# The first mixer: where POOL splits the query weights of the third and fourth group

## The chip, the core and the metric

The kernel runs on one core of a Trainium2 chip. The metric is device time in microseconds (us), the median of several executions. The engines are TensorE (PE in the profile, with its weight loads as PEld), VectorE (DVE), ScalarE (ACT), GpSimd (POOL) and SyncE (SP), whose queue issues the DMAs.

## The reference

The kernel computes two layers of an encoder trunk on 512 tokens of width 1024, in float32. Each layer is a token mixer with 12 heads in three key/value groups, beside 4 heads of attention to 256 memory tokens, and then a gated feed-forward part. The first layer's mixer is the banded one, with a sink logit per head:

```python
def reference(x, mem, ...):
    mem_n = rms_norm(mem, mem_norm_g)
    for i in range(DEPTH):
        h = rms_norm(x, g_mix_pre[i])
        proj = h @ w_in[i]                     # q | k | v | q for the memory heads
        ...
        tok = mixer_a(q, k, v, attn_sink[0], cos_p, sin_p)   # i = 0: |i - j| <= 128
        mkv = mem_n @ w_mem_kv[i]
        mo = memory_attention(qm, km, vm)
        o = jnp.concatenate([tok, mo], axis=-1) @ w_o[i]
        x = x + rms_norm(o, g_mix_post[i])
        h = rms_norm(x, g_ffn_pre[i])
        gu = h @ w_gate_up[i]
        f = (jax.nn.silu(gu[..., :D_FF]) * gu[..., D_FF:]) @ w_down[i]
        x = x + rms_norm(f, g_ffn_post[i])
    return x
```

In `mixer_a` the queries and keys get a rotary embedding on 16 of 64 dimensions, the scores get a band mask, and the softmax's denominator has the term of the sink.

## The kernel before

Every product of float32 matrices is made from three products of numbers split into a high part (rounded to TensorE's fp32r format) and a low part, the rest. A weight is loaded into a raw tile of 128 x 1024 by SP (`raw`, three buffers), and `split` makes `whi` (a copy in fp32r) and `wlo` (raw less `whi`), each with four buffers. `split` is told by a number of two bits who does it: with the bit of value 2 set POOL makes the high part (L284), else ScalarE (L286); with the bit of value 1 set POOL makes the low part (L288), else VectorE (L290). The table PACE holds these bits. For the query weights of the first layer they are `'qw': [0, 0, 0, 1, 3, 3, 3, 3]`, two entries for each of four groups of four heads: the halves of the third group and of the fourth (the four memory heads) are split by POOL alone, each in four instructions of 128 x 512, two copies and two subtractions (NPART is 2, so a half comes in two parts).

TensorE's order is fixed by hand. `mixer` puts each piece of work into a list with a position, in units of heads, and runs the list in that order. Head number hg has its four scores at hg, hg + 1/4 and so on, its turns (`turn`, transposes of the probabilities, L643) 1.69 later, and the products with the values (`value`, L657 and L658) half a head after these. The query products of groups 1 to 3 begin at 4c - 5 plus a small offset, that is at -0.8, 3.1 and 7.1. The other engines' instructions are ordered by the scheduler of the framework, by priority and by when their operands are expected.

For a head, VectorE adds the mask and takes the maximum (L588), ScalarE makes the exponentials `p` (L594), and `normalise` adds the sink's term to the denominator (L629, VectorE), takes the reciprocal `rd` (L630, VectorE) and multiplies the four pieces of `p` with it on POOL (L633). The turns wait for that. Between these instructions VectorE makes the rotary embedding of the next group's queries (`rope_a`: L440, L442 and L443, 128 x 64 elements each, with both inputs in SBUF), and the low part of these queries (L290, `q`). Before the heads, the memory's keys are made: `mem_pieces` leaves them in `k2`, POOL makes a second copy of the high part (`again`, L417), and `keys` transposes them for TensorE (L424, L429) with copies out of PSUM by ScalarE (L426) and VectorE (L430, `kmb`).

The raw tiles are used in turn, so that SP's load of a later unit waits until the split of the unit three places ahead is done (L230); SP's queue is in program order.

Of the kernel before, what the change touches and what calls it, by code (L numbers as in the profile page):

```python
# [13 lines left out]
OP = mybir.AluOpType  # L14
# [16 lines left out]
NPART = 2  # L31
WPART = 2
BIG = 1e37
NFILL = 3
URGENT = 150
FIRST = ((0, 0.05, 0.1, 0.15, 1, 1.5), (0.5, 0.55, 0.6, 0.65, 1.25, 1.75))
LATE = {2: 1.2, ("r", 0): 1.05, ("r", 1): 1.3, 3: 2.2, ("r", 2): 2.4, ("r", 3): 3.4, ("m", 0): 4.5, ("m", 1): 5,
        "rows": 4, ("rm", 0): 6, ("rm", 1): 6.2}
# [147 lines left out]
class Trunk:  # L186
    def __init__(self, tc, a):
        self.tc, self.nc, self.a, self.nraw, self.more, self.early = tc, tc.nc, a, 0, None, {}
        self.pairs, self.todo, self.stores = {}, [], []

    def pool(self, stack, name, side="left", **kw):
        return stack.enter_context(self.tc.tile_pool(name=name, bufs=1, side=side, reuse_waits="tile", **kw))
# [16 lines left out]
                                       for z in range(2)]  # L209
            self.stores = [(self.pairs[(name, *at)][z], pair[z].bitcast(F32)) for z in range(2)]  # L210

    def unit(self, src, side=0, pool=None, parts=1, put=None, x=0, dst=None, key=None, g=None, raw=None, pair=None, early=None):


        nc, n = self.nc, src.shape[-1]
        own = raw or self.early.pop(early, None)
        if pair in self.pairs:
            def fetch():
                dst[key] = [self.whl.tile([P, 1024], F32R, tag=z, name=f"w{z}", bufs=4) for z in ("hi", "lo")]
                for z in range(2):  # L220
                    nc.sync.dma_start(dst[key][z].bitcast(F32), self.pairs[pair][z])

            put(x, fetch)
            return

        def load():
            raw = own or self.raw()
            hi, lo = [(pool or self.whl).tile([P, 1024], F32R, tag=z, name=f"w{z}", bufs=4) for z in ("hi", "lo")]
            if not own:
                nc.sync.dma_start(raw[:, :n], src)  # L230
            return raw, hi, lo

        def part(t, c0, c1):
            raw, hi, lo = t
            if g is None:
                self.split(hi[:, c0:c1], lo[:, c0:c1], raw[:, c0:c1], side)
                return
            m = n // g.shape[1]
            for k in range(c0 // m, c1 // m):
                c = slice(k * m, k * m + m)  # L240
                if side & 1:
                    nc.gpsimd.tensor_scalar(raw[:, c], raw[:, c], g[:, k:k + 1], 1.0, op0=OP.mult, op1=OP.mult)
                else:
                    self.split_scaled(hi[:, c], lo[:, c], raw[:, c], g[:, k:k + 1], side)
            if side & 1:
                self.split(hi[:, c0:c1], lo[:, c0:c1], raw[:, c0:c1], side)

        if put is None:
            t = load()
            for z in range(parts):  # L250
                part(t, z * n // parts, (z + 1) * n // parts)
            return t[1:]
        box = []

        def first():
            box.append(load())
            dst[key] = box[0][1:]
            part(box[0], 0, n // NPART)

        put(x, first)  # L260
        for z in range(1, NPART):
            put(x + z / 4, lambda z=z: part(box[0], z * n // NPART, (z + 1) * n // NPART))

    def raw(self):

# [27 lines left out]
    def urgent(self):  # L293

        return self.tc.high_priority(URGENT)

# [219 lines left out]
    def q_pieces(self, l, c, qTs, put, x0, lead):  # L516
        nc = self.nc
        w = {}
        for z in range(2):
            self.unit(self.a["wq"][l, c, z], self.side(l, "qw", 2 * c + z), put=put, x=x0 - lead + z * lead / 3, dst=w,  # L520
                      key=z, pair=("wq", l, c, z), early=("wq", z) if l == c == 0 else None)

        def prod(t, st, u):
            self.ready(t)
# [98 lines left out]
    def normalise(self, hd):  # L623
        nc, sink, nm, den = self.nc, hd["sink"], hd["nm"], hd["den"]
        rd = self.small.tile([P, 4], F32, tag="rd", name="rd", bufs=4)
        if sink is not None:
            es = self.small.tile([P, 4], F32, tag="es", name="es", bufs=3)
            nc.scalar.activation(es, nm, AF.Exp, bias=self.sink[:, sink:sink + 1], scale=1.0)
            nc.vector.tensor_add(den, den, es)  # L629
        nc.vector.reciprocal(rd, den)  # L630
        for z, (k0, k1) in enumerate(hd["rng"]):
            n = (k1 - k0) * P
            self.pooled = nc.gpsimd.tensor_scalar(hd["p"][z][:, :n], hd["p"][z][:, :n], rd[:, z:z + 1], 1.0,  # L633
                                                  op0=OP.mult, op1=OP.mult)

    def turn(self, hd, j):
        nc = self.nc
# [45 lines left out]
    def mixer(self, l, mkp, late, tokp):  # L683
# [9 lines left out]
        def put(x, f):  # L693
            bisect.insort(items, (x, next(count), f), key=lambda z: (-z[0], -z[1]))
# [48 lines left out]
        for z, key in enumerate(list(late)):  # L743
            at = pc["late"] + z - (len(late) - 1) if l else LATE[key]
            put(xk + at * k, lambda key=key: self.ready(key))
        lay(self.kv_pieces(l), xk, k, pc["klag"], lambda t: 0 if l else max(0, t - 1) / 4, None if l else FIRST)
        lay(self.q_pieces(l, 0, qT, put, xq + pc["q0off"], pc["q0lead"]), xq + pc["q0off"], pc["q0step"], pc["q0lag"],
# [621 lines left out]
```

## Time and profile before

| | us |
|---|---|
| median of 3 runs | 1112.88 |
| lowest and highest run | 1111.99, 1113.64 |
| the profiled execution | 1110.48 |
| its span, first to last instruction | 1108.7 |
| TensorE busy | 1089.4 |
| VectorE busy | 840.7 |
| ScalarE busy | 658.5 |
| POOL busy | 196.2 |

The granted clock of TensorE is 0.999 over the span. The profiled execution took 1.78 us more than its span, and lies 2.40 us below the median of the runs. The first mixer's heads begin at about 56 us of the span and end at about 170. In the profile's lines, `x4` is the number of merged instructions, the arrow in brackets names what ended the idle time ahead of an instruction, and `L288` is a line of the kernel before.

### The profile page before, as it was taken

The numbers are of one execution on the slowest core, as the hardware profiler recorded it, in microseconds if no ns is written. First come the engines' busy times: TensorE is split into PE (matmuls) and PEld (weight loads), VectorE is DVE, ScalarE is ACT, GpSimd is POOL, SyncE is SP. The second block draws the span as 40 slices with busy tenths as digits, with TensorE's granted clock in tenths as the row PEclk, the third lists the DMA queues.
The fourth block names the chain that finished last, engine by engine and source line by source line (L and its number), as shares of the span: only waits on it lengthen the run. The fifth ranks groups of instructions, "written<-read, shape, count | busy, mean of one in ns | idle before, by whom it ended". The sixth has DMA issues, their size and how long they took to land.

```text
span 1108.7 us, 19514 instructions
## 1 busy us (share of the span) xinstructions
PE 1089.4 (98%) x7438; PEld 1000.2 (90%) x7438; DVE 840.7 (76%) x1433; ACT 658.5 (59%) x1356; POOL 196.2 (18%) x342
## 2 busy tenths in 40 slices
PE   8999999999999999999999999999999999999997
PEld 7989978999889989998898888879999899899986
DVE  7789875999558767875788988758995478669854
ACT  6679975765445534563567888756664366346631
POOL 5683331102000000000443542212000000000001
PEclk9999999999999999999999999999999999999999
DMA  8621017343833472325543221145136123322243
GB/s 319 224 98 40 25 33 266 115 153 127 308 116 108 152 248 76 115 92 189 186 143 114 77 77 38 39 172 171 59 112 213 56 95 115 134 72 98 82 168 114
DMA packets 40558, 142.44 MB, mean 128 GB/s; under 512 B 4624, under 2 KB 5008, under 8 KB 40336
## 3 DMA queue, kind: packets, MB, share of 16 engines
q1 hardware_dynamic: 40176, 140.66, 36.8%
q8 instruction: 58, 0.95, 0.4%
q10 hardware_dynamic: 288, 0.53, 0.2%
q14 instruction: 36, 0.29, 0.1%
HBM read 122.30 MB, written 18.87 MB: 127 GB/s over the span
## 4 chain that ended last, share of the span: by engine, by line
PE 88%; DVE 5%; ACT 2%; POOL 2%; issue 1%; DMA 1%; DVEq 0%; POOLq 0%; SPq 0%; ACTq 0%
PE ps L277 14%; PE ps L276 14%; PE ps L278 14%; PE ps L1042 12%; PE ps L1041 12%; PE ps L1040 12%; PE tp L643 3%; PE o L658 2%; PE o L657 2%; PE s L582 1%; PE s L583 1%; DVE tl L290 1%; POOL r L310 1%; DVE tok L666 1%; ACT junk L314 1%
## 5 line engine op out<-in xcount | busy, mean ns | idle before, releaser
L286 ACT ACTIVATE whi<-raw 128x1024 fp32r<-128x1024 f32 (+3 forms) x205 | 168.5, 839 | 176.9 <-PE ps L1042 73.5
L290 DVE TENSOR_TENSOR wlo<-raw,whi 128x1024 fp32r<-128x1024 f32 (+3 forms) x202 | 190.9, 960 | 73.5 <-ACT whi L286 71.5
L1041 PE MATMUL ps<-sf,wlo 128*128 128x256 f32 x640 | 179.8, 281 | 0.0
L1040 PE MATMUL ps<-sf,whi 128*128 128x256 f32 x640 | 179.7, 281 | 0.0
L1042 PE MATMUL ps<-sf,whi 128*128 128x256 f32 x640 | 179.7, 281 | 0.0
L276 PE MATMUL ps<-whi,f 128*128 128x512 f32 (+1 forms) x360 | 138.7, 385 | 0.0
L277 PE MATMUL ps<-wlo,f 128*128 128x512 f32 (+1 forms) x360 | 138.5, 385 | 0.0
L278 PE MATMUL ps<-whi,f 128*128 128x512 f32 (+1 forms) x360 | 138.4, 385 | 0.0
L1042 PE MATMUL ps<-a,whi 128*128 128x256 f32 x480 | 134.4, 280 | 0.0
L1040 PE MATMUL ps<-a,whi 128*128 128x256 f32 x480 | 134.4, 280 | 0.0
L1041 PE MATMUL ps<-a,wlo 128*128 128x256 f32 x480 | 133.8, 279 | 0.0
L1041 PEld LDWEIGHTS ps<-sf,wlo 128*128 128x128 f32 x640 | 121.4, 190 | 0.5
L1040 PEld LDWEIGHTS ps<-sf,whi 128*128 128x128 f32 x640 | 121.1, 189 | 0.5
L1042 PEld LDWEIGHTS ps<-sf,whi 128*128 128x128 f32 x640 | 121.4, 190 | 0.0
L319 POOL TENSOR_SCALAR e<-sso 128x1 f32<-128x1 f32 x8 | 3.4, 420 | 563.9 <-ACT junk L314 563.7
L276 PE MATMUL ps<-whi,hT 128*128 128x256 f32 (+1 forms) x312 | 95.2, 305 | 0.0
L633 POOL TENSOR_SCALAR p<-p,rd 128x256 f32<-128x256 f32 (+2 forms) x128 | 76.5, 615 | 101.0 <-DVE rd L630 43.2
L277 PE MATMUL ps<-wlo,hT 128*128 128x256 f32 (+1 forms) x312 | 91.1, 292 | 2.9 <-DVE wlo L290 2.9
L278 PE MATMUL ps<-whi,hT 128*128 128x256 f32 (+1 forms) x312 | 90.9, 291 | 0.0
L1041 PEld LDWEIGHTS ps<-a,wlo 128*128 128x128 f32 x480 | 90.5, 188 | 0.2
L1040 PEld LDWEIGHTS ps<-a,whi 128*128 128x128 f32 x480 | 90.4, 188 | 0.2
L1042 PEld LDWEIGHTS ps<-a,whi 128*128 128x128 f32 x480 | 90.1, 188 | 0.0
(209 smaller groups left out, 2703.6 us busy)
## 6 DMA issues: line engine op xcount, KB each, us to landing
raw<-in_wgu_dram SPq DMA_DIRECT2D x48, 512.0 KB, 4.3
raw<-in_wd_dram SPq DMA_DIRECT2D x44, 512.0 KB, 4.4
rb<-in_wgu_dram SPq DMA_DIRECT2D x40, 512.0 KB, 3.6
raw<-in_wo_dram SPq DMA_DIRECT2D x17, 512.0 KB, 3.7
raw<-in_wq_dram SPq DMA_DIRECT2D x16, 512.0 KB, 5.3
xt<-x SPq DMA_DIRECT2D x12, 512.0 KB, 4.7
raw<-in_wm_dram SPq DMA_DIRECT2D x8, 512.0 KB, 4.0
x<-y SPq DMA_DIRECT2D x8, 512.0 KB, 3.0
```

The lines of the kernel that those rows point to most:

```text
L276: mm(out, lh, rh, start=first, stop=False)
L277: mm(out, lh, rl, start=False, stop=False)
L278: mm(out, ll, rh, start=False, stop=last)
L286: a = nc.scalar.activation(hi, src, AF.Copy)
L290: b = nc.vector.tensor_sub(lo, src, hi.bitcast(F32))
L633: self.pooled = nc.gpsimd.tensor_scalar(hd["p"][z][:, :n], hd["p"][z][:, :n], rd[:, z:z + 1], 1.0, op0=OP.mult, op1=OP.mult)
L643: nc.tensor.transpose(tp[:, z], hd["p"][i][:, jj * P:(jj + 1) * P], self.ident)
L657: nc.tensor.matmul(o[:, c0:c1], hd["v"](j), th, start=(j == 0), stop=False, skip_group_check=True)
L658: nc.tensor.matmul(o[:, c0:c1], hd["v"](j), tl, start=False, stop=last, skip_group_check=True)
L1040: mm(out, wh[:, s], rh, start=start and k == 0, stop=False, skip_group_check=True)
L1041: mm(out, wl[:, s], rh, start=False, stop=False, skip_group_check=True)
L1042: mm(out, wh[:, s], rl, start=False, stop=k == 3, skip_group_check=True)
```

## The change

The splits of the four halves are each tied to a normalising: the third group's halves come behind that of heads 0 and 1, and the fourth group's behind that of heads 3 and 4. `normalise` keeps its last POOL instruction of every head, and both parts of a half are issued within `issue_after` of that instruction, which sets the order of the two and does no more. Only the first layer has entries.

```diff
+BEHIND = {(0, 2, 0): 0, (0, 2, 1): 1, (0, 3, 0): 3, (0, 3, 1): 4}
...
+        def behind(c0, c1):
+            with nullcontext() if after is None else self.tc.issue_after(self.pooled[after].ins):
+                part(box[0], c0, c1)
+
         def first():
             box.append(load())
             dst[key] = box[0][1:]
-            part(box[0], 0, n // NPART)
+            behind(0, n // NPART)
 
         put(x, first)
         for z in range(1, NPART):
-            put(x + z / 4, lambda z=z: part(box[0], z * n // NPART, (z + 1) * n // NPART))
+            put(x + z / 4, lambda z=z: behind(z * n // NPART, (z + 1) * n // NPART))
...
-                      key=z, pair=("wq", l, c, z), early=("wq", z) if l == c == 0 else None)
+                      key=z, pair=("wq", l, c, z), early=("wq", z) if l == c == 0 else None, after=BEHIND.get((l, c, z)))
...
-            self.pooled = nc.gpsimd.tensor_scalar(hd["p"][z][:, :n], hd["p"][z][:, :n], rd[:, z:z + 1], 1.0,
-                                                  op0=OP.mult, op1=OP.mult)
+            self.pooled[hd["hg"]] = nc.gpsimd.tensor_scalar(hd["p"][z][:, :n], hd["p"][z][:, :n], rd[:, z:z + 1], 1.0,
+                                                            op0=OP.mult, op1=OP.mult)
```

In the changed kernel every line behind the new table is a few lines further on. The first place is POOL's queue at the first heads. `k2_824` and `k2_855` are the two tiles of memory keys; `raw_1083` and `raw_1134` the halves of the third group's weights; `rd_941` and `rd_1035` the reciprocals of heads 0 and 1. Before:

```order
L417 TENSOR_SCALAR k2_824<-k2_824 128x4x64 [waits DVE_49,Activation_49]
L284 TENSOR_SCALAR whi_1084<-raw_1083 128x512 [waits DMAHW4_49]
L284 TENSOR_SCALAR whi_1084<-raw_1083 128x512
L288 TENSOR_TENSOR wlo_1085<-raw_1083,whi_1084 128x512 [waits Pool_49] x2
L284 TENSOR_SCALAR whi_1135<-raw_1134 128x512 [waits DMAHW5_49,DVE_49,PE_49]
L284 TENSOR_SCALAR whi_1135<-raw_1134 128x512
L417 TENSOR_SCALAR k2_855<-k2_855 128x4x64 [waits Activation_49]
L288 TENSOR_TENSOR wlo_1136<-raw_1134,whi_1135 128x512 [waits Pool_49] x2
L633 TENSOR_SCALAR p_884<-p_884,rd_941 128x256 [waits DVE_49,Activation_49]
```

And now:

```order
L422 TENSOR_SCALAR k2_824<-k2_824 128x4x64 [waits DVE_49,Activation_49]
L422 TENSOR_SCALAR k2_855<-k2_855 128x4x64 [waits DVE_49,Activation_49]
L638 TENSOR_SCALAR p_884<-p_884,rd_941 128x256 [waits DVE_49,Activation_49]
L638 TENSOR_SCALAR p_899<-p_899,rd_941 128x384 [waits Activation_49]
L638 TENSOR_SCALAR p_914<-p_914,rd_941 128x384 [waits Activation_49]
L638 TENSOR_SCALAR p_938<-p_938,rd_941 128x256 [waits Activation_49]
L289 TENSOR_SCALAR whi_1084<-raw_1083 128x512 [waits DMAHW4_49]
L289 TENSOR_SCALAR whi_1084<-raw_1083 128x512
L293 TENSOR_TENSOR wlo_1085<-raw_1083,whi_1084 128x512 [waits Pool_49] x2
L638 TENSOR_SCALAR p_979<-p_979,rd_1035 128x256 [waits DVE_49,Activation_49]
```

Both halves of the third group stood ahead of head 0's normalising, with the second tile of memory keys between them. Now the memory keys and head 0 come first, and each half stands behind one head. In the same way the fourth group's halves, which stood between heads 1 and 2 but for one subtraction behind head 2, now stand behind heads 3 and 4.

The second place is TensorE's queue at the first product with the second half of the third group's weights (`whi_1135`, `wlo_1136`); `o_1221` is head 1's output. Before:

```order
L657 MATMUL o_1221<-th_1209,vs_246 128x384 [waits Activation_49]
L658 MATMUL o_1221<-tl_1210,vs_246 128x384 [waits DVE_49]
L276 MATMUL ps_1214<-whi_1135,hT_116 128x256
L277 MATMUL ps_1214<-wlo_1136,hT_116 128x256
L278 MATMUL ps_1214<-whi_1135,hT_118 128x256
```

And now:

```order
L662 MATMUL o_1221<-th_1209,vs_246 128x384 [waits Activation_49]
L663 MATMUL o_1221<-tl_1210,vs_246 128x384 [waits DVE_49]
L281 MATMUL ps_1214<-whi_1135,hT_116 128x256 [waits Pool_49]
L282 MATMUL ps_1214<-wlo_1136,hT_116 128x256 [waits Pool_49]
L283 MATMUL ps_1214<-whi_1135,hT_118 128x256
```

No row has moved there; the two products have a wait of their own on POOL, which an earlier wait had covered. VectorE's, ScalarE's and SP's queues have the same rows in the same order as before.

More of the change, by code (lines that the diff above doesn't have):

```diff
@@ L188, in __init__ @@
         self.tc, self.nc, self.a, self.nraw, self.more, self.early = tc, tc.nc, a, 0, None, {}
-        self.pairs, self.todo, self.stores = {}, [], []
+        self.pairs, self.todo, self.stores, self.pooled = {}, [], [], {}
     def pool(self, stack, name, side="left", **kw):
@@ L210, in ahead, with unit @@
             self.stores = [(self.pairs[(name, *at)][z], pair[z].bitcast(F32)) for z in range(2)]
-    def unit(self, src, side=0, pool=None, parts=1, put=None, x=0, dst=None, key=None, g=None, raw=None, pair=None, early=None):
+    def unit(self, src, side=0, pool=None, parts=1, put=None, x=0, dst=None, key=None, g=None, raw=None, pair=None, early=None, after=None):
         nc, n = self.nc, src.shape[-1]
```

## The prediction

> **What bounds the kernel now.** I read the page first. Its first part says that TensorE is busy for nearly the whole span, so the time falls only where TensorE stands idle, or where one of its waits goes away.
>
> ```profile
> PE 1089.4 (98%) x7438; PEld 1000.2 (90%) x7438; DVE 840.7 (76%) x1433; ACT 658.5 (59%) x1356; POOL 196.2 (18%) x342
> ```
>
> The change touches the first mixer alone, so next I asked for the busy time of each engine in stretches around the first heads. The columns are busy us of PE, PEld, DVE, ACT and POOL, each with its count, then clock and DMA.
>
> ```profile
> 56.00:62.50 6.50, 5.30 (x47) 5.19 (x46) 6.15 (x16) 4.88 (x14) 6.00 (x8) 1.00 0.51 185
> 62.50:67.00 4.50, 3.71 (x29) 3.20 (x29) 4.37 (x14) 2.73 (x9) 3.35 (x5) 1.00 0.42 136
> 67.00:79.00 12.00, 12.00 (x100) 11.90 (x101) 9.72 (x31) 10.22 (x31) 9.26 (x14) 1.00 0.13 44
> 79.00:86.00 7.00, 6.60 (x50) 5.81 (x49) 6.04 (x21) 5.48 (x16) 4.32 (x7) 1.00 0.29 92
> 86.00:100.00 14.00, 14.00 (x115) 13.79 (x114) 12.05 (x41) 12.41 (x37) 4.77 (x10) 1.00 0.00 1
> ```
>
> TensorE's idle time is 1.20 us in the first stretch, 0.79 in the second and 0.40 in the fourth, and nothing in the others: 2.39 us in all. That is the most that this part of the program can give. VectorE is at 6.15 of 6.50 and 4.37 of 4.50 in the first two stretches: it is the engine that TensorE runs behind there. The list of waits says for whom.
>
> ```profile
> PEld tp L429 <- POOL k L417: 1.3, 1, 1.3
> PE tp L429 <- DVE kmb L430: 1.2, 1, 1.2
> ...
> PE tp L643 <- POOL p L633: 0.8, 2, 0.4
> ```
>
> The wait of 1.2 us stands before the second transposes of the second tile of memory keys: their weights come from POOL's copy (L417), and their PSUM buffer is freed by VectorE (L430). The two waits of 0.4 stand before head 0's turns, which need POOL's normalising (L633).
>
> Now what POOL and VectorE do there, from their timelines (start, duration, engine, line, what). POOL:
>
> ```profile
> 56.51 1.21 POOL L284 TENSOR_SCALAR whi<-raw 128x512 fp32r<-128x512 f32 x2 [0.85 <-DMA raw<-in_wq_dram]
> 57.67 2.59 POOL L288 TENSOR_TENSOR wlo<-raw,whi 128x512 fp32r<-128x512 f32 x2
> 60.23 1.19 POOL L284 TENSOR_SCALAR whi<-raw 128x512 fp32r<-128x512 f32 x2
> 61.40 0.57 POOL L417 TENSOR_SCALAR k<-k 128x256 fp32r<-128x256 f32 x1
> 61.93 2.53 POOL L288 TENSOR_TENSOR wlo<-raw,whi 128x512 fp32r<-128x512 f32 x2
> 65.61 2.22 POOL L633 TENSOR_SCALAR p<-p,rd 128x256 f32<-128x256 f32 x4 [1.15 <-DVE rd L630]
> 70.56 2.24 POOL L633 TENSOR_SCALAR p<-p,rd 128x256 f32<-128x256 f32 x4 [2.73 <-DVE qx L442]
> 72.80 1.21 POOL L284 TENSOR_SCALAR whi<-raw 128x512 fp32r<-128x512 f32 x2
> ...
> 78.92 2.24 POOL L633 TENSOR_SCALAR p<-p,rd 128x256 f32<-128x256 f32 x4
> ```
>
> VectorE, and the spread of its rotary lines over the first mixer (minimum, median and maximum in ns):
>
> ```profile
> 58.17 0.92 DVE L442 TENSOR_TENSOR qx<-qx,cst 128x64 f32<-128x64 f32 x1
> ...
> 59.56 0.78 DVE L443 TENSOR_TENSOR qx<-qx,rt 128x64 f32<-128x64 f32 x1
> ...
> 60.88 0.81 DVE L290 TENSOR_TENSOR q<-qx,q 128x256 fp32r<-128x256 f32 x1
> ...
> 62.62 0.67 DVE L440 TENSOR_TENSOR rt<-qx,cst 128x64 f32<-128x64 f32 x1
> 63.33 1.22 DVE L442 TENSOR_TENSOR qx<-qx,cst 128x64 f32<-128x64 f32 x1
> ...
> 65.27 0.16 DVE L630 RECIPROCAL rd<-den 128x4 f32<-128x4 f32 x1
> ...
> 70.08 0.23 DVE L440 TENSOR_TENSOR rt<-qx,cst 128x64 f32<-128x64 f32 x1
> 70.22 0.17 DVE L630 RECIPROCAL rd<-den 128x4 f32<-128x4 f32 x1
> ...
> 76.86 0.17 DVE L630 RECIPROCAL rd<-den 128x4 f32<-128x4 f32 x1
> ...
> 77.79 1.23 DVE L442 TENSOR_TENSOR qx<-qx,cst 128x64 f32<-128x64 f32 x1
> ```
>
> ```profile
> L440 DVE TENSOR_TENSOR rt<-qx,cst x12: 193/218/669, 32.8 to 104.6; 128x64 f32<-128x64 f32 x12
> L442 DVE TENSOR_TENSOR qx<-qx,cst x12: 206/224/1226, 35.0 to 105.2; 128x64 f32<-128x64 f32 x12
> L443 DVE TENSOR_TENSOR qx<-qx,rt x12: 211/288/781, 35.4 to 105.9; 128x64 f32<-128x64 f32 x12
> L290 DVE TENSOR_TENSOR q<-qx,q x5: 412/440/815, 60.9 to 87.1; 128x256 fp32r<-128x256 f32 x5
> ```
>
> This is the central reading. The same 128x64 instruction takes 0.22 us as a rule and 0.92, 1.22 and 1.23 us at three places, and each of the three lies beside one of POOL's subtractions (57.67 to 60.26, 61.93 to 64.46, the one that ends where the 78.92 row begins). The long ones end just after a POOL instruction ends: 63.33 + 1.22 = 64.55 against 64.46, and 77.79 + 1.23 = 79.02 against 78.92. So VectorE's instructions with both inputs in SBUF stood still until POOL's current one was over. The Trainium skill has this in "SBUF — State Buffer", Who interferes with whom: a VectorE instruction with two SBUF inputs and a GpSimd instruction that reads SBUF exclude each other, and whichever starts second waits for the whole of the first. By that rule the trace agrees, 1.22 us against 0.22.
>
> **The change part by part.** It adds and removes no work: POOL's 16 split instructions, its copies and its normalising stay, and the order of TensorE, VectorE, ScalarE and SP is the same row for row; TensorE gains only waits on POOL.
>
> *POOL between 56.5 and 64.5 us becomes nearly empty.* The second copy of memory keys follows the first at once instead of starting at 61.40, and head 0's normalising comes next. What VectorE gets back ahead of its first `kmb` copy is 0.92 - 0.22 = 0.70, 0.78 - 0.29 = 0.49 and 0.81 - 0.44 = 0.37, together 1.56 us; the wait of TensorE is 1.20. ScalarE stands between: it must finish the second exponential of head 0 before it makes `q`'s high part, so I let VectorE's gain count for 1.0 to 1.2 and take 1.1 of TensorE's 1.20 us. The copy by POOL, which ended at 61.97 before, is then some 5 us early, so it is not what is late next.
>
> *Head 0's normalising.* Ahead of the reciprocal at 65.27, VectorE also gets back 0.67 - 0.22 = 0.45 and 1.22 - 0.22 = 1.00, so 3.0 us in all. TensorE arrives at the turns 1.1 us earlier, and would have to have the reciprocal 1.1 + 0.79 = 1.9 us earlier to lose both waits. Between those 3.0 and this 1.9 lie ScalarE's exponentials, which VectorE must wait for; I put the reciprocal 2.1 us earlier. So the whole 0.8 goes: at 67 us TensorE is 1.9 us ahead.
>
> *The moved splits of the third group.* One set costs POOL 1.21 + 2.59 = 3.80 us by the first rows. In the old clock less 1.9, head 0 is normalised until about 65.7, the first set runs until 69.5, head 1's follows as soon as its reciprocal is there (70.22 less 1.9 is 68.3, so it waits for POOL about 1.2 us), until 71.8, and the second set until 75.6. Who needs what:
>
> ```profile
> 73.25 0.38 PE L643 MATMUL tp<-cst,p 128*128 128x128 f32 x2
> ...
> 76.19 0.36 PE L276 MATMUL ps<-whi,hT 128*128 128x256 f32 x1
> ...
> 80.28 0.28 PE L276 MATMUL ps<-whi,hT 128*128 128x256 f32 x1
> ```
>
> 73.25 is head 1's first turn; 76.19 and 80.28 are the first uses of the two halves of the third group's weights. Less 1.9 they come at 71.4, 74.3 and 78.4. The weights are ready at 69.5 and 75.6: 4.8 and 2.8 us to spare. The first two of head 1's four pieces (about half of 2.24) are ready at 69.6 + 1.1 = 70.7, with 0.7 to spare. So no wait of TensorE is added directly.
>
> *Indirectly*, the first set's last subtraction (68.2 to 69.5) meets the rotary instructions behind head 1's denominators, which began with L440 at 70.08 and come at about 68.2. One of them is held for up to 1.3 us, and VectorE and ScalarE then lose most of what they had gained, for one head. TensorE's own slack (the 0.7 above; a turn's two PSUM buffers) takes most of it; I charge 0.1 us, with 0 and 1.3 as the ends.
>
> *Head 2.* Its reciprocal was ready at 77.03, but POOL began at 78.92, since the splits of the memory heads' weights lay ahead; and L442 stood for 1.23 us. Both go, since these two sets now lie behind heads 3 and 4. The 0.40 us of the stretch from 79 to 86 is the consequence, of which I take 0.35.
>
> *The sets behind heads 3 and 4* fall into POOL's gaps:
>
> ```profile
> 85.09 2.05 POOL L633 TENSOR_SCALAR p<-p,rd 128x256 f32<-128x256 f32 x4 [2.68 <-DVE rt L440]
> 91.67 2.10 POOL L633 TENSOR_SCALAR p<-p,rd 128x256 f32<-128x256 f32 x4 [4.53 <-ACT th L286]
> 98.47 2.06 POOL L633 TENSOR_SCALAR p<-p,rd 128x256 f32<-128x256 f32 x4 [4.70 <-DVE rt L440]
> ```
>
> From 87.14 to 91.67 and from 93.77 to 98.47 there are 4.53 and 4.70 us for 3.80. They meet one `q` subtraction each, held for at most the 0.6 us of one high-part instruction; VectorE is at 12.05 of 14.00 there, so I cost this at nothing (0 to 0.6). Their weights are used from head 7 on. SP's loads that wait for these raw buffers come later by as much as the splits, some 9 to 14 us. One is the second half of the memory heads' weights, free to load at 69.5 and split behind head 4; the next is the first unit of the output projection, split only here:
>
> ```profile
> 101.23 1.14 ACT L286 ACTIVATE whi<-raw 128x512 fp32r<-128x512 f32 x2
> ```
>
> Its buffer is free at about 75.6, so over 20 us of cover remain.
>
> **Sum**: -1.1 - 0.8 - 0.35 + 0.1 = -2.15 us. The profiled execution took 1110.48 us with a span of 1108.7, and the median of the runs is 2.40 above it; TensorE is busy for 98% of the span, so the gain should last to the end: 1110.48 - 2.15 = 1108.3 for the profiled execution, and 1112.88 - 2.15, about 1110.7, for the median.
>
> **Rivals.** *Given back at head 1*: the lock moves with the splits instead of going. If one subtraction holds L440, which stands ahead of head 1's reciprocal, and the slack of 0.7 is used up, TensorE loses 1.3 - 0.7 = 0.6 there in place of the 0.1 charged, and VectorE comes to head 2 as late as before, so that the 0.35 stays: -2.15 + 0.5 + 0.35 = -1.3, about 1111.6. For it speaks that the held instructions come once per head, just at the reciprocal; against it, that TensorE's slack is real in the stretch from 67 to 79, which has no idle time though POOL is busy for most of it. By the skill's rule on the port above, this is the rule that speaks against the change: a split moved beside other rotary instructions holds those.
>
> *Not what it says*: VectorE's long instructions have another cause, or ScalarE sets the pace of head 0; then the early waits only change name: 1112.9.
>
> *Slower*: at all four new places both L440 and L442 are held, 2 x 1.30 = 2.6 us. From head 1's reciprocal (70.39) to its first turn (73.25) there are 2.86 us, of which 1.1 are two normalising pieces, so 1.7 of slack; the rest, 0.9, falls on TensorE four times, 3.6 - 2.15: about 1114.3. It decides from the point where a head's rotary group loses over 1.7 us. Against it: a group of three short instructions would have to start inside two subtractions in turn, and the sets behind heads 3 and 4 end before the next head's group.
>
> **How the numbers follow.** Forecast 0.60, given back 0.24, not what it says 0.08, slower 0.08. The 0.2% that a measurement can tell is 2.2 us, so the forecast lies on that edge: a little over half of its chance counts as faster, 0.33, and 0.05 of the second case, 0.38 together. Slower takes its own 0.08 and 0.02 of the third, 0.10; 0.52 are left for no change. The range: all 2.39 us and the half width of the runs (1111.99 to 1113.64, 0.8) give 1109.7 below; the third case with half of that above, 1113.3. The slower case is left out.
>
> **What would show it.** Right: L442 near 0.22 us in head 0, no wait before L429, none before head 0's turns, TensorE's head 2 turn about 2 us earlier. Wrong: long L440 or L442 beside the moved splits with a TensorE wait on `tl` behind them, a wait for `whi` or `wlo` at the third group's products, or the same lengths as before with POOL idle beside them.

## The result and the profile after

| | before | after |
|---|---|---|
| median of 20 runs each, in turn | 1112.23 us | 1109.80 us |
| lowest and highest | 1110.59, 1113.86 | 1109.43, 1111.45 |
| ratio, with its 95% interval | | 0.9981 (0.9974 to 0.9988) |
| profiled execution, span | 1110.48, 1108.7 | 1110.09, 1108.3 |

The median fell by 2.4 us, a little more than the 2.15 us of the sum. But the two profiled executions differ by only 0.39 us: that of the changed kernel took 1110.09 us, where the prediction had 1108.3. Both numbers are right. The executions of the kernel before spread over a shorter and a longer group that touch each other. An execution is counted as long here when it lies over 1.2 us above the shortest of the same kernel in its session: 64 of 130 are long over all the comparisons below, and 2 of 31 of the changed kernel's. Where the granted clock of TensorE is on record for each, its mean is 0.9974 in the long ones of the kernel before and 0.9987 in the short ones. Six executions of these comparisons that took 1328 to 5391 us are left out of all counts. Both profiles are of short executions. So there are two things to explain: 0.9 us between the short ones (their medians are 1110.6 to 1110.8 and 1109.8), and why the long ones are nearly gone.

First the profile. The same stretches as before the change, in the same columns:

```profile
56.00:62.50 6.50, 6.50 (x59) 6.44 (x58) 5.64 (x20) 5.72 (x17) 0.46 (x2) 1.00 0.36 144
62.50:67.00 4.50, 4.50 (x40) 4.47 (x39) 3.62 (x15) 4.18 (x13) 3.55 (x7) 1.00 0.00 0
67.00:79.00 12.00, 11.64 (x91) 10.88 (x90) 11.24 (x31) 9.01 (x27) 10.36 (x14) 1.00 0.29 89
79.00:86.00 7.00, 6.67 (x53) 6.20 (x52) 6.07 (x21) 5.95 (x18) 2.38 (x5) 1.00 0.00 1
86.00:100.00 14.00, 13.97 (x109) 12.95 (x108) 12.21 (x39) 11.67 (x35) 11.55 (x16) 1.00 0.24 76
```

TensorE's idle time in the first two stretches is gone, 1.99 us. But there is new idle time of 0.36 us from 67 to 79, and the count of PE's rows in the last stretch fell from 115 to 109: TensorE is busy there by the modelled ends of its products and yet gets through less. A busy column that stays full is no proof that nothing was lost; the start of each head's first score is a better clock. The table is read from PE's rows of the two traces. The last row is the difference less 0.39, since the profiled execution of after came 0.39 us later to head 0, for reasons ahead of the change.

| head | 0 | 1 | 2 | 3 | 4 | 5 | 6 | 7 | 8 | 9 |
|---|---|---|---|---|---|---|---|---|---|---|
| before | 56.05 | 62.79 | 69.03 | 75.70 | 82.66 | 90.04 | 96.76 | 103.43 | 110.58 | 117.24 |
| after | 56.44 | 61.94 | 66.97 | 73.65 | 81.17 | 88.56 | 95.74 | 102.84 | 110.08 | 116.77 |
| gained since head 0 | 0 | 1.24 | 2.45 | 2.44 | 1.88 | 1.87 | 1.41 | 0.98 | 0.89 | 0.86 |

2.45 us are gained by head 2, and then 0.56, 0.46 and 0.43 are given back between the first scores of heads 3 and 4, of heads 5 and 6, and of heads 6 and 7. What was gained is seen on VectorE and POOL (start, duration, engine, line, what):

```profile
58.57 0.22 DVE L447 TENSOR_TENSOR qx<-qx,cst 128x64 f32<-128x64 f32 x1
...
62.16 0.23 DVE L447 TENSOR_TENSOR qx<-qx,cst 128x64 f32<-128x64 f32 x1
...
63.11 0.17 DVE L635 RECIPROCAL rd<-den 128x4 f32<-128x4 f32 x1
```

The instructions that took 0.92 and 1.22 us are back at 0.22, and head 0's reciprocal is 2.16 us earlier (2.55 counted from head 0). What was given back stands at four other places of VectorE:

```profile
68.07 1.38 DVE L445 TENSOR_TENSOR rt<-qx,cst 128x64 f32<-128x64 f32 x1
...
74.55 1.10 DVE L634 TENSOR_TENSOR den<-den,es 128x4 f32<-128x4 f32 x1
...
85.66 0.89 DVE L295 TENSOR_TENSOR q<-qx,q 128x256 fp32r<-128x256 f32 x1
...
92.73 0.89 DVE L295 TENSOR_TENSOR q<-qx,q 128x256 fp32r<-128x256 f32 x1
```

Each lies beside one of POOL's moved splits:

```profile
66.83 2.55 POOL L293 TENSOR_TENSOR wlo<-raw,whi 128x512 fp32r<-128x512 f32 x2
...
73.10 2.53 POOL L293 TENSOR_TENSOR wlo<-raw,whi 128x512 fp32r<-128x512 f32 x2
...
85.66 1.38 POOL L289 TENSOR_SCALAR whi<-raw 128x512 fp32r<-128x512 f32 x2
...
92.73 1.38 POOL L289 TENSOR_SCALAR whi<-raw 128x512 fp32r<-128x512 f32 x2
```

The second is the plainest: an addition of 128x4 elements, 0.16 us as a rule, stood for 1.10 us until POOL's subtraction was over at 75.63. It is the sum ahead of head 2's reciprocal.

### The profile page after: what moved, and what is told of

It is laid out like the page before. It is cut to its first block, busy times and chain, and to the rows that moved or that the text cites. A ratio compares the mean times of both kernels' runs of the same rounds, so it can differ in the third digit from the quotient of the medians.

```text
span 1108.3 us, 19517 instructions
## 1 busy us (share of the span) xinstructions
PE 1090.3 (98%) x7438; PEld 1000.2 (90%) x7438; DVE 840.7 (76%) x1433; ACT 658.9 (59%) x1356; POOL 196.3 (18%) x342
## 4 chain that ended last, share of the span: by engine, by line
PE 87%; DVE 5%; ACT 3%; POOL 2%; issue 1%; DMA 1%; DVEq 0%; POOLq 0%; SPq 0%; ACTq 0%
PE ps L282 14%; PE ps L281 14%; PE ps L283 14%; PE ps L1045 12%; PE ps L1047 12%; PE ps L1046 12%; PE tp L648 3%; PE o L662 2%; PE o L663 2%; PE s L587 1%; PE s L588 1%; DVE tl L295 1%; POOL r L315 1%; PE tp L563 1%; ACT p L599 1%
```

## The experiments

The port theory is that of the prediction: a VectorE instruction with both inputs in SBUF is held until POOL's instruction beside it ends. Its first rival was that a load or POOL's own order makes the waits; later rivals are named in the expectations. Medians are of 11 or 12 runs, beside the kernel before in the same session; the changed kernel itself ran in the first comparison and in the session of after_again.

| kernel | median | before beside it | ratio (95%) |
|---|---|---|---|
| third_group | 1112.47 | 1111.05 | 1.0012 (1.0002 to 1.0022) |
| fourth_group | 1111.21 | 1111.05 | 0.9998 (0.9989 to 1.0007) |
| copy_first | 1110.63 | 1111.05 | 0.9998 (0.9989 to 1.0007) |
| before_again | 1111.19 | 1111.05 | 1.0006 (0.9997 to 1.0015) |
| after_again | 1109.82 | 1111.60 | 0.9987 (0.9978 to 0.9995) |
| filled | 1111.61 | 1111.60 | 1.0002 (0.9994 to 1.0011) |
| dummy_sub | 1112.06 | 1111.60 | 1.0005 (0.9996 to 1.0013) |
| gated | 1113.26 | 1111.60 | 1.0018 (1.0010 to 1.0027) |
| spread | 1110.63 | 1111.09 | 0.9996 (0.9987 to 1.0005) |
| pieces | 1108.92 | 1111.09 | 0.9978 (0.9969 to 0.9987) |
| unmoved | 1110.30 | 1112.29 | 0.9989 (0.9979 to 0.9999) |

**The third group alone** (third_group).

```diff
-BEHIND = {(0, 2, 0): 0, (0, 2, 1): 1, (0, 3, 0): 3, (0, 3, 1): 4}
+BEHIND = {(0, 2, 0): 0, (0, 2, 1): 1}
```

> Only the third group's halves are moved (behind heads 0 and 1); the fourth group's splits stay where the scheduler puts them, now 7 POOL instructions ahead of head 2's normalising. The port theory (VectorE's instructions with both inputs in SBUF are held by POOL's subtractions): head 0's waits go as in the changed kernel, TensorE is about 1.9 us ahead at head 1, but head 2's normalising begins only at about 81 us of the span and its first turn loses 2 us or more, so 0 to +1 us against the kernel before. The arrival theory (in most runs of the kernel before, the load of the third group's first half lands later than in the profiled one, and the copy and head 0's normalising slide behind it in POOL's queue): the runs lie together within 1 us, without the two clusters of the kernel before, and the median is up to 2 us lower than a port theory alone gives.

The waits ahead of head 0 went, and head 2 began at 66.73 us, as in the changed kernel. Then it lost all of it, and the median came out 1.4 us above that of the kernel before, more than the 0 to 1 us expected. The fourth group's splits now stood in POOL's queue right behind the third's, ahead of head 2's normalising, and TensorE's rows say who was late; the stretches after them (busy us of PE, PEld, DVE, ACT and POOL, clock, DMA) say what followed:

```profile
79.62 0.44 PE L663 MATMUL o<-tl,vs 128*128 128x384 f32 x1 [1.22 <-DVE tl L295]
82.11 1.04 PE L648 MATMUL tp<-cst,p 128*128 128x128 f32 x2 [1.33 <-POOL p L638]
```

```profile
78.00:80.00 2.00, 0.78 (x5) 0.46 (x4) 2.00 (x3) 0.69 (x2) 2.00 (x3) 1.00 0.08 33
80.00:82.00 2.00, 0.78 (x7) 0.57 (x5) 1.33 (x6) 1.35 (x4) 2.00 (x3) 0.85 0.85 252
82.00:84.00 2.00, 1.80 (x7) 1.51 (x8) 0.27 (x1) 0.45 (x2) 2.00 (x5) 0.50 0.04 14
```

TensorE idled for 2.44 us out of four, and from about 81.4 to 88.2 us, by the clock of these and the following stretches, it ran at half its clock. So the third group's part is worth nothing by itself: POOL's queue passes the delay on to the next head.

**The fourth group alone** (fourth_group), with the other two entries of the table only.

> Only the fourth group's halves are moved (behind heads 3 and 4). Port theory: head 0's waits of 1.2 and 0.8 us stay; head 2 gains 0.35, and the two query subtractions held behind heads 3 and 4 cost 0.45 each as in the changed kernel: +0.3 to +0.6 us. Arrival theory: the same, and the runs still fall into two clusters about 2 us apart, as in the kernel before.

```profile
62.49 0.50 PE L434 MATMUL tp<-identr,k 128*128 128x128 f32 x4 [1.22 <-DVE kmb L435]
66.18 0.33 PE L648 MATMUL tp<-cst,p 128*128 128x128 f32 x1 [0.39 <-POOL p L638]
```

The early waits stay, head 2's normalising no longer queues (it begins at 77.03 instead of 78.92), which brings 0.77 us by head 5's first score, and this is given back by head 8's. Alone it is worth nothing either; its use is that it makes room for the third group's.

**Only the order of POOL's copy** (copy_first). The third group's halves stay ahead of head 0, but behind POOL's second copy of the memory keys.

```diff
-BEHIND = {(0, 2, 0): 0, (0, 2, 1): 1, (0, 3, 0): 3, (0, 3, 1): 4}
+BEHIND = {(0, 2, 0): ("k2", 1), (0, 2, 1): ("k2", 1)}
...
-            self.again(k2)
+            self.pooled["k2", m] = self.again(k2)
```

> The third group's halves stay ahead of head 0's normalising but come behind the second copy of memory keys; nothing else is moved. If that copy's place in POOL's queue is the cause of the wait of 1.2 us: that wait goes and head 0's stay, about -1 us. Port theory: TensorE waits for VectorE's copy out of PSUM instead, since VectorE's three instructions are held as before; the wait stays within 0.3 us and the time within 0.3 us. Arrival theory: two clusters of runs as before.

The copy was done by 58.6 us, and TensorE waited as before; this execution is 1.7 us late from its start, where the clock stood at 0.60 and 0.54 between 14 and 18 us.

```profile
64.46 0.51 PE L434 MATMUL tp<-identr,k 128*128 128x128 f32 x4 [1.51 <-DVE kmb L435]
68.51 0.33 PE L648 MATMUL tp<-cst,p 128*128 128x128 f32 x1 [0.39 <-POOL p L638]
```

So the wait that the list of waits puts beside POOL's copy is VectorE's, and VectorE's is that of the hold.

**The two kernels again** (before_again and, in the next session, after_again).

> The kernel before, for a second profile and more runs. Arrival theory: the runs fall into two clusters, near 1110.7 and 1112.8 us; in a profile of the upper cluster POOL's first split of the third group begins later than 56.5 us, with a longer wait for its load. Port theory alone: in such a profile the load lands at the same time and other VectorE instructions are held.

> The changed kernel once more, in the same session as the three runs beside it. Both theories expect a median near 1109.8 us. Clock theory (some runs of the kernel before are longer because TensorE, which idles 1.2 and 0.8 us close together between 61 and 67 us there, falls to half of its clock for a few us afterwards; the changed kernel has no such idle): nearly all of its runs lie in one cluster between 1109.4 and 1110.4, while a third or more of those of the kernel before lie above 1111.5. Chance theory (the longer runs come from the start of the program, whatever stands at 61 to 67 us): the share of longer runs is alike in both kernels, a third or more here too.

The profile of before_again is of a short execution too (1111.19 us), with POOL's wait for the load at 0.87 us against 0.85 before, so it can't tell whether a later load makes the long ones; filled, below, speaks against that. In the session of after_again 19 of 33 executions of the kernel before were long, and 1 of 11 of the changed kernel. Alike shares, which the chance theory asks for, were not measured: most of the long executions go with something that the change takes away.

**TensorE's idle time filled** (filled).

```diff
+    def fill(self, n):
+        for _ in range(n):
+            self.nc.tensor.matmul(self.spare[:, 256:], self.identr, self.ka[:, 0, :256], start=True, stop=True,
+                                  skip_group_check=True)
...
+        if n == 4 and t == 1 and self.more is None:
+            self.spare = self.ps.tile([P, 512], F32, tag="acc", name="ps", bufs=2)
+            self.fill(10)
...
+            if hd["hg"] == 0 and j == 0 and hd["sink"] is not None:
+                self.fill(3)
```

> The kernel before, order of POOL's work untouched, with 16 extra products on TensorE whose results nobody reads, put where it idles: 10 between the first and the second half of the second memory-key tile's work, 3 each ahead of head 0's second and fourth transposes. The waits of VectorE and POOL stay. Clock theory: the time of an undisturbed run stays near 1110.6 to 1111, since the waits are still there, but the longer runs are gone or rare, so the median falls from 1111 to 1112 to about 1110.8. Chance theory: a third or more of the runs stay above 1111.5, the median as before or up to 1 us worse for the extra work.

The extra products write into the bank in which the third query tile of group 1 is summed, and change that tile's values. Long executions fell from 19 of 33 to 2 of 11, as the clock theory says, though the loads and POOL's splits are ordered as they were. The short ones, 1111.5, came out 0.9 us longer than those of the kernel before (0.72 us by head 4's first score, counted from head 0), more than expected, so the median gained nothing.

**POOL busy with data that nobody needs** (dummy_sub).

```diff
+            ins = self.again(k2)
+            if l == 0 and m == 1:
+                jk = self.core.tile([P, 2, 256], F32, tag="jk", name="jk", bufs=1)
+                with self.tc.issue_after(ins.ins):
+                    for _ in range(5):
+                        nc.gpsimd.tensor_tensor(jk, self.mT[:, 0, 0:2].bitcast(F32), self.mT[:, 1, 0:2].bitcast(F32), op=OP.subtract)
```

> The changed kernel with five POOL subtractions of 128x512 between two tiles of SBUF into a third that nobody reads, put behind POOL's copy of the second memory-key tile, where the third group's splits stood before: work of POOL on data that nothing waits for. Port theory (a VectorE operation with two operands in SBUF is held while POOL's reading instruction runs): the waits of 1.2 us at the second memory-key tile and of about 0.8 us ahead of head 0's turns come back, the time rises 1 to 2.5 us above the changed kernel. Rival (it was the weights' arrival or the splits' own data that made those waits): VectorE is not held, and only POOL's normalising of head 0 is later, by what of the five is left at 63.1 us; the rise is then below 1 us unless that normalising is late.

The median is 2.2 us above that of the changed kernel. POOL's five subtractions, one of VectorE's instructions beside them, and TensorE's wait:

```profile
57.12 6.81 POOL L418 TENSOR_TENSOR jk<-mT 128x512 f32<-128x512 f32 x5
```

```profile
58.82 1.05 DVE L452 TENSOR_TENSOR qx<-qx,cst 128x64 f32<-128x64 f32 x1
```

```profile
63.54 0.50 PE L439 MATMUL tp<-identr,k 128*128 128x128 f32 x4 [2.02 <-DVE kmb L440]
```

The hold needs nothing of the weights: these subtractions of other data do it too. Head 0's normalising was not held up by POOL's queue (it began at 65.33, right after its reciprocal at 64.99), and the waits ahead of head 0's turns, expected back too, did not come: the one wait of 2.02 us is all. And this profile shows what a wait of that size does to TensorE's clock, in the column ahead of the last two:

```profile
62.00:64.00 2.00, 0.46 (x5) 0.49 (x6) 2.00 (x5) 1.55 (x5) 1.85 (x2) 1.00 0.00 0
64.00:66.00 2.00, 2.00 (x14) 2.00 (x14) 1.87 (x9) 1.51 (x5) 0.67 (x2) 0.57 0.03 8
66.00:68.00 2.00, 2.00 (x11) 2.00 (x11) 0.71 (x3) 1.59 (x4) 2.00 (x4) 0.57 0.00 0
```

Four microseconds at 0.57 are 4 x 0.43 / 0.5 = 3.4 us at half clock and cost 1.7 us, about what separates the long executions of the kernel before from its short ones (medians by session 1112.2 to 1112.9 against 1110.6 to 1110.8).

**A gate ahead of the fourth group's splits** (gated).

```diff
+            if l == 0 and c == 2:
+                gate = self.small.tile([P, 1], F32, tag="gate", name="gate", bufs=2)
+                self.gates.append(nc.gpsimd.tensor_scalar(gate, st["q2"][:, 0, HD:HD + 1].bitcast(F32), 1.0, 1.0,
+                                                          op0=OP.mult, op1=OP.mult))
...
+                with self.tc.issue_after(self.gates[after - 3].ins) if after in (3, 4) else nullcontext():
```

> The changed kernel with one more tiny POOL instruction (128x1) ahead of each of the two splits of the fourth group's weights, reading the low part of the third group's tile, so that these splits begin only after VectorE's subtraction has written it. Port theory (VectorE's subtraction of 128x256 took 0.89 instead of 0.41 us at 85.7 and 92.7 us because POOL's instruction of the split ran beside it): both take about 0.41 again, heads 3 to 4 and 5 to 6 come about 0.45 us sooner each, in all 0.9 us off the changed kernel, some 1109.0. Rival (the time is set elsewhere by then, by the weights or by POOL): the subtractions get shorter but the time stays within 0.2 us of the changed kernel, or the later splits hold up the fourth group by up to 1 us.

VectorE's two subtractions took 0.42 and 0.41 us again. But the splits, 0.6 us later now counted from head 0, met the next instruction with two inputs, the denominators of the head behind (POOL, VectorE, TensorE):

```profile
87.62 2.54 POOL L294 TENSOR_TENSOR wlo<-raw,whi 128x512 fp32r<-128x512 f32 x2
```

```profile
89.47 0.71 DVE L639 TENSOR_TENSOR den<-den,es 128x4 f32<-128x4 f32 x1
```

```profile
91.40 0.41 PE L653 MATMUL tp<-cst,p 128*128 128x128 f32 x2 [0.21 <-DVE qx L448]
98.62 0.41 PE L653 MATMUL tp<-cst,p 128*128 128x128 f32 x2 [0.38 <-DVE tl L296]
```

At head 9 the gated kernel is where the changed one was (60.29 us behind head 0 against 60.33): the hold was moved and not removed, which a median alone would have told as the rival's case. Most of the 3.4 us in its median come much later, in the feed-forward part, where no instruction was changed: from 785 to 845 us TensorE makes 500 products in 60 us there and 505 in the changed kernel, both without a break. The median expected, 1109.0, was missed by 4.3 us.

**The fourth group's work in VectorE's gaps** (spread). The tiny instruction writes into the split's own tile; the two copies come behind head 3, one half's subtractions behind head 4, the other's behind head 5.

```diff
+                with self.urgent():
+                    if after == 3:
+                        self.gated = self.gate(hi, self.q2s[2, 0], 3)
+                with self.tc.issue_after(self.gated), self.urgent():
+                    for c in halves:
+                        nc.gpsimd.tensor_scalar(hi[:, c], raw[:, c], 1.0, 1.0, op0=OP.mult, op1=OP.mult)
+                with self.tc.issue_after(self.gate(lo, self.q2s[2, after - 2], after + 1)):
+                    for c in halves:
+                        nc.gpsimd.tensor_tensor(lo[:, c], raw[:, c], hi[:, c].bitcast(F32), op=OP.subtract)
```

> The changed kernel with the fourth group's work put into the gaps between VectorE's two-input instructions: a tiny POOL instruction (128x1, into the split's own tile) reads the low part of the third group's tile and so waits for VectorE's subtraction; behind head 3 both copies in fp32r (2.4 us), behind head 4 the first subtractions (2.5 us), behind head 5 the second (2.5 us). From VectorE's subtraction to its next denominators there are 3.4 us, which a whole set of 3.75 us doesn't fit. Port theory: no VectorE instruction is held between 84 and 104 us, and TensorE's waits behind heads 3 to 6 that the changed kernel added go: 0.7 to 0.9 us less, 1108.9 to 1109.1. Rival (those waits have another cause, since with the gate alone they only moved by one head): the same 1109.8.

Counted from head 0, TensorE was 0.85 us ahead of the changed kernel at head 7's first score, the size that the port theory gave. At head 8's it was 0.44 us behind: the last subtractions met VectorE's own split of an output weight, which I had not looked for (POOL, VectorE, TensorE):

```profile
99.51 2.99 POOL L271 TENSOR_TENSOR wlo<-raw,whi 128x512 fp32r<-128x512 f32 x2
```

```profile
100.24 2.81 DVE L312 TENSOR_TENSOR wlo<-raw,whi 128x512 fp32r<-128x512 f32 x2
```

```profile
103.44 0.55 PE L667 MATMUL tp<-cst,p 128*128 128x128 f32 x3 [0.48 <-DVE tl L312]
```

VectorE's pair takes 1.29 us alone; here the engines took turns.

**Shorter instructions** (pieces), the changed kernel but for this:

```diff
-            with nullcontext() if after is None else self.tc.issue_after(self.pooled[after].ins):
-                part(box[0], c0, c1)
+            with self.tc.issue_after(self.pooled[after].ins):
+                for c in range(c0, c1, 256):
+                    part(box[0], c, c + 256)
```

> The changed kernel, its four moved splits issued by POOL in instructions of 128x256 instead of 128x512, twice as many of half the length; all the other engines' orders are the same. Port theory (a VectorE instruction with both inputs in SBUF waits for the end of the POOL instruction beside it): no hold can be longer than about 0.7 us; the holds of 1.38 us at 68.1, 1.10 us at 74.6 and the two of 0.89 us at 85.7 and 92.7 us get shorter, and TensorE gets back some of the 1.5 us that it lost between 77 and 100 us: 0.4 to 0.8 us less than the changed kernel, some 1109.2. Rival (the holds last as long as POOL has such work in a row, whatever its instructions' lengths): the holds stay, the time is that of the changed kernel or a little more for POOL's longer work.

```profile
67.80 0.51 DVE L449 TENSOR_TENSOR rt<-qx,cst 128x64 f32<-128x64 f32 x1
...
73.89 0.16 DVE L638 TENSOR_TENSOR den<-den,es 128x4 f32<-128x4 f32 x1
...
84.31 0.67 DVE L299 TENSOR_TENSOR q<-qx,q 128x256 fp32r<-128x256 f32 x1
```

```profile
67.00:79.00 12.00, 12.00 (x99) 11.87 (x97) 11.20 (x34) 9.46 (x29) 11.35 (x21) 1.00 0.28 87
```

None of the instructions held beside the moved pieces takes longer than 0.68 us, the idle time from 67 to 79 is gone (99 rows of PE instead of 91), and the median is 0.9 us below the changed kernel's of the other sessions and 2.2 us below that of the kernel before beside it: the best version here. The gain is all at one place, between heads 3 and 4. The fourth group's sets cost no less: of the 2.91 us gained on the kernel before at head 5's first score 1.77 are left at head 7's, 1.1 lost against 0.9 in the changed kernel, as the shorter pieces now also meet the denominators of the heads behind (0.60 us at 88.19 and 0.48 at 95.51 for 0.16). POOL pays for it with 4.3 us a set instead of 3.8.

**Shorter instructions at the old places** (unmoved).

```diff
+        def pieces(c0, c1):
+            step = 256 if pair in [("wq", 0, c, z) for c in (2, 3) for z in range(2)] else c1 - c0
+            with self.tc.issue_after(self.copied) if pair == ("wq", 0, 2, 1) else nullcontext():
+                for c in range(c0, c1, step):
+                    part(box[0], c, c + step)
```

> The kernel before with the splits left at their places and only issued in POOL instructions of 128x256; POOL's second copy of the memory keys comes between the third group's two halves, the other engines' orders are the same. It tells the length of POOL's instructions from their place. Length theory (what VectorE loses is the rest of the one instruction it meets): the holds of 0.92, 0.78, 0.81, 0.67, 1.22 and 1.23 us fall to at most 0.7, VectorE gets back about half of its 3.0 us ahead of head 0, the waits of 1.2 and 0.8 us shrink to about 0.5 and 0.3, and the time of the runs at full clock falls by about 1.2 us to some 1109.5. Rival (place is what counts: with POOL busy without a break, each of VectorE's two-input instructions is held by one piece after another): VectorE loses as much, the waits stay near 2 us together and the time stays at 1110.5 to 1111 for the runs at full clock.

The length theory was right about VectorE, whose reciprocal of head 0 came at 64.01 us, 1.26 us earlier than before. The rival was nearer with the time: POOL's own queue was still full, so that the normalising began at 65.95, and TensorE waited for it (VectorE, POOL, TensorE):

```profile
64.01 0.17 DVE L636 RECIPROCAL rd<-den 128x4 f32<-128x4 f32 x1
```

```profile
64.34 1.62 POOL L294 TENSOR_TENSOR wlo<-raw,whi 128x256 fp32r<-128x256 f32 x2
65.95 2.05 POOL L639 TENSOR_SCALAR p<-p,rd 128x256 f32<-128x256 f32 x4
```

```profile
61.95 0.50 PE L435 MATMUL tp<-identr,k 128*128 128x128 f32 x4 [0.66 <-POOL whi L290]
66.48 0.33 PE L649 MATMUL tp<-cst,p 128*128 128x128 f32 x1 [1.23 <-POOL p L639]
```

The waits are 2.1 us together, as in the kernel before, and its short executions (median 1110.2) are 0.5 us shorter than those of before (1110.7).

**One look more at the kernel before** (before_look).

> The kernel before once more, for its profile. If this execution is one of the longer ones (above 1111.5 us), clock theory expects a granted clock of about 0.5 for some 3 us right behind the waits at 61 to 67 us, and full clock before them; chance theory expects such a stretch at the start of the program or elsewhere. If it is one of the shorter ones, the clock is full throughout, and the run tells nothing.

It took 1110.6 us at full clock, a short one, and tells nothing. So no profile of a long execution of the kernel before was had. What stands for the clock theory is the count of long ones against TensorE's idle time in that place. With the waits of about 2 us in the kernel (before, fourth_group, copy_first, unmoved) 76 of 163 executions are long; with none between 61 and 67 us (changed, pieces, spread, gated, filled) 9 of 76. Left out of the count are third_group and dummy_sub, in whose profiled executions the clock fell; by the same measure 7 of 11 and 1 of 11 of theirs are long.

The traces speak against the theory in its simple form. In every one of them the granted clock changes only at times that lie whole multiples of 3.413 us apart (in third_group 22 and then 2 of them), and these times lie elsewhere in each execution. The one profile of a long execution with waits of about 2 us is that of copy_first (1113.38 us). Four such periods of it, in the columns of the stretches above:

```profile
11.01:14.42 3.41, 1.86 (x9) 1.07 (x9) 3.41 (x9) 1.48 (x5) 3.05 (x6) 1.00 0.71 249
14.42:17.83 3.41, 3.41 (x11) 3.41 (x12) 2.89 (x9) 2.12 (x6) 2.31 (x6) 0.50 1.02 373
62.20:65.62 3.42, 1.91 (x19) 1.80 (x19) 3.38 (x9) 3.03 (x11) 3.42 (x5) 1.00 0.53 158
65.62:69.03 3.41, 3.00 (x23) 2.49 (x22) 3.31 (x12) 2.24 (x6) 2.26 (x5) 1.00 0.50 153
```

The clock fell behind 1.55 us of idle time at the start of the program, and stayed full behind the whole wait of 1.51 us at the memory keys; besides the 1.7 us at the start, this execution lost 1.2 us at about 850 us, and nothing more than the short ones behind the waits. Behind the wait of 1.22 us in fourth_group, all of it in the period from 59.36 to 62.77, the clock stayed full too. The other falls came behind periods with 1.83 us (third_group) and 2.02 us (dummy_sub) of idle time, and the waits of the kernel before, as profiled, put no more than 1.2 us into any 3.413 us. So waits of that size were not seen to lower the clock, and what makes its long executions stays open.

## Why the prediction was right in the time and half right in the steps

*The memory keys' wait and the waits before head 0's turns* (1.1 + 0.8 = 1.9 predicted): right in kind, and too small. 2.45 us were gained by head 2. The waits' own idle time was 2.0; the rest is that behind each wait of 0.4 us TensorE issued a transpose alone, 0.74 and 0.72 us from start to start in place of 0.18 and 0.14. The two parts of the cause that the prediction saw were both needed: unmoved shows that VectorE's early reciprocal is worth nothing while the splits fill POOL's queue.

*Head 1's rotary group, 0.1 charged, and head 2's 0.35 gained*: 0.25 us less was predicted, and 0.56 more measured, between the first scores of heads 3 and 4. The hold at L445 was there (1.38 us), as foreseen, and TensorE's slack took it. What failed is the list of places: the second subtraction, behind head 1's normalising, met the denominators of head 2 (1.10 us for 0.16), which the prediction hadn't counted among VectorE's instructions with two inputs. pieces shows it: with that addition at 0.16 us, 0.8 us came back by 77 us.

*The sets behind heads 3 and 4, costed at nothing (0 to 0.6)*: this is the step that failed. They cost 0.46 and 0.43 and some 0.1 at head 7, 1.0 us together. Spread took away the holds and got 0.85 us of it, before it lost it elsewhere. The reason given, that VectorE had time over in that stretch (12.05 of 14.00), was no reason: the transposes of the queries (L563) wait for just that subtraction, and stood 0.31 and 0.28 us behind the product ahead of them instead of 0.12, with the turn ahead of the first of them (0.27 instead of 0.12) late as well: 0.5 us together, the rest in smaller steps beside them. A busy share says nothing of the slack of one chain.

Together 0.9 us at full clock instead of 2.15: the rival "given back at head 1" (-1.3) had the better sum, though most of it was given back at other heads.

*The median* fell by 2.4 all the same, since half of the executions of the kernel before were also some 1.5 to 2.3 us longer, and nearly none of the changed kernel's were. No step of the prediction had that: that the sum and the fall of the median lie so close together is luck, and the profiled execution, forecast at 1108.3, took 1110.09. The mean clocks, 0.9974 against 0.9987, fit some 2.9 us more at half clock in a long execution, by an estimate from these two and 1110 us. The Trainium skill, "TensorE: Matmul & The Clock Gate", Part 1: The HAM clock gate, says that TensorE's clock falls to half after an idle window of about 3.4 us, and that these windows run on their own, so that the same kernel meets them differently from run to run. The second agrees with the traces: the changes of the clock lie whole multiples of 3.413 us apart, at other places in each execution, and it stood at half for one such window in dummy_sub and for two in third_group. The first asks for more idle time than the runs did: the clock fell behind windows with 1.55, 1.83 and 2.02 us of idle time. The measurement decides: a window that is idle for about half of its length can be enough, while windows with up to 1.54 us left the clock full (filled and unmoved, near 14 us). The waits of the kernel before were not seen to reach that. That its long executions come from there is argued from the counts and from filled, the profiles of copy_first and fourth_group speak against it, and the cause of this larger part of the median's fall stays open.

## What to carry to other kernels

An engine pair that locks each other out is a matter of instruction lengths: cut the low-priority side into short pieces as well as looking for a better place, since a VectorE instruction lost at most 0.46 us to pieces of 0.39 and 0.71 us (pieces), against 1.16 to wholes of 0.6 and 1.27; and move it if it also stands in a queue ahead of something urgent. Pieces make POOL's work longer, though, and can meet instructions that the whole had passed: they brought 0.9 us at the third group and nothing at the fourth. For each new place of a moved instruction, list every instruction of the other engine with two inputs that passes there, down to the smallest, and ask of each who waits for it. When the median and one profile disagree, look at the single executions and at the granted clock of each before explaining either.

## What was not expected of the hardware

- Two engines' subtractions on SBUF data that overlap take turns: POOL's pair took 2.99 us instead of 2.54 and VectorE's 2.81 instead of 1.29 (spread).
- A wait of 1.22 us and the first 0.6 us of the next (third_group), one of 2.02 us (dummy_sub), or 1.55 us at the start of the program (copy_first) were enough for the clock to fall to half, for 6.8, 3.4 and 3.4 us; one of 1.51 us was not (copy_first).
- One more tile of 128x1 in SBUF went with a feed-forward part in which the products take about 1% longer on average and none of them is long by itself (gated, 3 us in all from 750 to 1090 us); spread, with gates of the same kind at other places and no new tile, has 505 products in that stretch again. The two rows, of gated and of after:

```profile
785.00:845.00 60.00, 60.00 (x500) 59.61 (x499) 53.99 (x78) 35.58 (x60) 0.00 (x0) 1.00 0.37 119
```

```profile
785.00:845.00 60.00, 60.00 (x505) 59.53 (x504) 53.62 (x78) 34.71 (x60) 0.00 (x0) 1.00 0.39 123
```

Whether the place of the tiles in SBUF is the cause was not tried.
